# Ordering depthwise taps behind key chains, and moving seven taps per tile to ScalarE and adding transfers, in a two-layer hybrid trunk

## The chip, the core and the metric

The kernel runs on one core of one Trainium2 chip. The metric is device time in microseconds (us), lower is better. PE stands for TensorE (matrix products; PEld its weight loads), DVE for VectorE, ACT for ScalarE, POOL for GpSimd, SP for SyncE, which here only issues transfers.

## What is computed

Two layers (l = 0 and 1, "first" and "second" here) over 256 latent and 256 context tokens of 1024 channels, all in float32. The part of the reference that matters:

```python
h = modulate(rmsnorm(x, norm1_g[l]), sh1, sc1)
p = h @ w_in[l]                       # columns: GLU, q, k, v, gates
u = a * sigmoid(g)                    # conv_branch: a, g are the GLU halves, 512 channels
u = dwconv1d(u, dw, dw_b)             # centred depthwise convolution, width 31
u = silu(layernorm(u, ln_g, ln_b))
y_conv = u @ w_o
q, k = rope_2d(q), rope_2d(k)         # latent tokens only
y_attn = neighbourhood_attention(q, k, v, k_ctx, v_ctx, rpb) @ w_na_out
x = x + g1 * ((sigmoid(g_conv) * y_conv + sigmoid(g_attn) * y_attn) @ w_out)
h2 = modulate(rmsnorm(x, norm2_g[l]), sh2, sc2)
x = x + g2 * conv_ffn(h2)
```

Attention: four rows of 64 columns; a query sees the keys of a window of 16 columns in each row, and all 256 context keys. In the second layer the context tokens only give keys and values.

## The kernel before

**Weights and products.** Every float32 product is made of three products of two parts (`mm3`, L196 to L199): the weight's high part times the activation's high and low part, and the weight's low part times the activation's high part. A weight unit is a tile of 128 x 1024, 512 KB. `raw_unit` (L152) loads it by SP into one of four buffers `raw`; ACT rounds it into `whi` (L167, L216). The low part `wlo` is made in one of two ways: `wunit` has DVE subtract (L168); `wadded` (L211) has ACT write the negated high part (L217) and POOL issue a transfer that adds the raw tile into it (L218). The set `ADDED` (L47) names the units, by layer and unit number, that take the second way. In the second layer these are three: q tiles 1 and 2 and gate 2.

**Groups and slots.** Activations lie transposed: channels on the 128 partitions, tokens along the free dimension, 512 of them in the first layer (latent and context), 256 in the second. `group` (L201) makes one output tile of 128 channels in a PSUM bank of the pool "main" (four banks): 8 x 3 products. At its end, and for 512 tokens once in its middle, it calls `slot()` (L92), which advances every registered side job by one step. The side jobs are the convolution's taps, the attention's steps, the layer norm and the modulation's dot products.

**The convolution.** `glu` (L687) writes a padded tile `u` per 128 channels (four tiles, j = 0 to 3) and appends its 31 taps to the list `taps`. A tap (L667) is one DVE instruction over the tile: the first writes `cb[j]` with scale and bias (L671), the others multiply a shifted view of `u` by one weight per partition and add it into `cb[j]` (L673). `conv_run` takes `rate` (2 or 3) taps per slot. When attention is done, `layer_norm` (L938) takes the rest, 5 or 6 per slot, then adds the four tiles (L949 and L950, in the second layer on POOL; L951 on DVE), sums over partitions on PE (L955), centres (L958), squares (L352, L356), and makes the reciprocal root with PE (L370), DVE (L378), POOL (L380) and PE (L386). Its output feeds the branch products of `w_conv_out` (L996).

**Queries and keys.** `qk(j)` (L843) is called for four pairs of heads. For q, then for k, it makes a group, rotates the latent part (DVE: L859, L860, L861, then L864 for q or L869 for k) and splits the results into high and low part (ACT L881, DVE L882). Keys are stored in three ranges: context (256 elements, straight from PSUM), and two ranges of 4 rows x 40 columns = 160 elements each, for the left and right half of the queries, with the columns outside. So a key chain ends with three casts and three subtractions. The queue of DVE steps from L859 to the last L882 is called a chain here. After both, `att.pair` registers the pair; the score products (L495) follow in a later slot, then bias and row maximum (DVE L516), exponentials (ACT L519) and scaling (L522), transposition (PE L561, copied by ACT L564 or L567) and the values (PE L578, L587; ACT L595, DVE L596).

**Order.** Each engine runs its own instructions in order. That order is a plan made when the program is built: instructions are taken in the order in which the code creates them, but one that is expected to be ready may be put ahead of one that is expected to wait. `tc.issue_after(i)` ties what is created inside it behind instruction i on the same engine, without a wait. The variable `after` (L658) holds the instruction behind which later taps are tied: the scores' L516 (or L530) sets it, so that taps don't stand ahead of scores. Nothing ties taps to the query and key chains.

Of the kernel before, what the change touches and what calls it, by code (L numbers as in the profile page):

```python
# [8 lines left out]
F32 = mybir.dt.float32  # L9
# [3 lines left out]
ALU = mybir.AluOpType  # L13
AX = mybir.AxisListType

P = 128
# [27 lines left out]

U_GLU0, U_V, U_IN, U_NA, U_CO, U_WO, U_UP, U_DN = 0, 2, 6, 36, 40, 44, 52, 96
NU = 118
ADDED = {*((0, U_IN + i) for i in (*range(19), 20, 22, 24, 26, 28)), *((0, u) for u in (U_NA + 1, U_NA + 3, *range(U_CO, U_CO + 4))), *((1, U_IN + i) for i in (7, 8, 16))}  # L47
T_GLU, T_Q, T_K, T_GATE = 0, 6, 10, 14

SWAP16 = [(i + 16) % 32 for i in range(32)]  # L50

# [2 lines left out]
def trunk(ctx: ExitStack, tc: tile.TileContext, xt, cvec, crow, wall, wada, params, bias_t, rope_t, out):  # L54
# [368 lines left out]
    class Attention:  # L423
# [147 lines left out]
        def values(self, what, js, pT, bank):  # L571
# [19 lines left out]
            for n, j in enumerate(js):  # L591
# [3 lines left out]
                act.copy(to[0], src)  # L595
                dve.tensor_tensor(to[1], src, to[0].bitcast(F32), ALU.subtract)  # L596

    def blocks(ap):
        return ap.rearrange("p (r b c) -> p b r c", r=ROWS, b=NB_)

# [31 lines left out]
    for l in range(DEPTH):  # L632
# [5 lines left out]
        with ExitStack() if last else start as e1a:  # L638
# [19 lines left out]
            after = [None]  # L658

            def conv_tap(j, t):  # L660
                if after[0] is not None:
                    with tc.issue_after(after[0].ins):
                        tap(j, t)
                else:
                    tap(j, t)

            def tap(j, t):  # L667
# [4 lines left out]
                else:  # L672
                    dve.scalar_tensor_tensor(cb[j], src, w, cb[j], ALU.mult, ALU.add)  # L673

            rate = [0.0]

            def conv_run():
                due = 0.0
# [33 lines left out]

            with ExitStack() as e1b:
                eb = e1b.enter_context(tc.tile_pool(name=f"eb{l}", bufs=1))
                V = [eb.tile([P, CONV], F32, name=f"V{l}_{t}") for t in range(2)]
                VW = eb.tile([P, NB_, CONV], F32, name=f"VW{l}")
                att = Attention(l, eb, T, V, VW, oh, ol, after)
# [125 lines left out]
                def qk(j):  # L843

                    att.ahead(j - 2)
                    bt = eb.tile([P, 5, NS_ // 2], F32, tag="bias", bufs=2 if last else 1, name=nm("bias"))
                    both = []
                    for what in range(2):
                        w = T if what == 0 else 2 * S
                        sc = HD ** -0.5 if what == 0 else 1.0  # L850
                        ps = in_group((T_Q, T_K)[what] + j, slice(0, w))
                        if what == 0:
                            with tc.issue_after(lastdma[0].ins):
                                sp.dma_start(bt, bias_t[l, j])
                        r1, r2 = tmp(), tmp()
                        got = back(ps[:, :w])
                        lat, ctx_ = (got[:, 0], got[:, 1]) if w > S else (got, None)
                        part = halves if w == S else lambda a: a
                        dve.tensor_tensor(part(r1[:, LAT]), lat, part(rope[:, 0, :]), ALU.mult)  # L859
                        dve.stream_shuffle(part(r2[:, LAT]), lat, SWAP16)  # L860
                        dve.tensor_tensor(r2[:, LAT], r2[:, LAT], rope[:, 1, :], ALU.mult)  # L861
                        if what == 0:
                            rq = tmp()
                            dve.tensor_tensor(  # L864
                                rq[:, LAT].rearrange("p (b r c) -> p b r c", b=NB_, r=ROWS),
                                blocks(r1[:, LAT]), blocks(r2[:, LAT]), ALU.add,
                            )
                        else:
                            dve.tensor_tensor(r1[:, LAT], r1[:, LAT], r2[:, LAT], ALU.add)  # L869
                        f = eb.tile([P, 2, KN if what else w], F32R, tag="qk"[what], bufs=2, name=nm("qk"))  # L870
                        if what == 0:
                            to = [([f[:, a, LAT] for a in range(2)], rq[:, LAT])]
                            if T > S:
                                to.append(([f[:, a, CTX] for a in range(2)], ctx_))
                        else:
                            rv_ = r1[:, LAT].rearrange("p (r c) -> p r c", r=ROWS)
                            to = [([f[:, a, KCTX] for a in range(2)], ctx_)]
                            for d, c in ((slice(0, KL), slice(GW - TC, GW)), (slice(KX, KN), slice(0, TC))):
                                to.append(([f[:, a, d].rearrange("p (c r) -> p r c", r=ROWS) for a in range(2)], rv_[:, :, c]))
                        for (hi, lo), src in to:  # L880
                            act.activation(hi, src, AF.Identity, scale=sc)  # L881
                            end = dve.scalar_tensor_tensor(lo, src, sc, hi.bitcast(F32), ALU.mult, ALU.subtract)  # L882
                        both.append(f)
                    att.pair(j, *both, bt, end)

# [39 lines left out]
            with ExitStack() as e1c:  # L925
# [12 lines left out]
                def layer_norm():  # L938
# [5 lines left out]
                        yield  # L944
                    pace[0] = 1.0 if last else 1.2
                    flat = [c.rearrange("p s t -> p (s t)") for c in cb]
                    sm = tp.tile([P, 512], F32, tag="ss", name=nm("ss"))
                    eng = pool if last else dve
                    eng.tensor_tensor(sm[:, :T], flat[0], flat[1], ALU.add)  # L949
# [407 lines left out]
```

## Time and profile before

| what | value |
|---|---|
| median of 3 runs (lowest, highest) | 1058.18 us (1057.49, 1059.27) |
| profiled execution: time, span | 1054.58 us, 1052.8 us |
| granted PE clock, mean over the span | 0.997 |
| second layer's taps on DVE, first and last tile's first tap | 688.2 us, 791.2 us |

A line of the grouped view reads: source line, engine, operation, output <- inputs, shapes, count | busy us, mean ns of one | idle time of the engine just before, and what ended it. A line of the waits view reads: engine and line that waited <- engine and line that ended the wait: total us, times, longest. A line of the timeline reads: start us, duration us, engine, line, operation, names, shapes, count. A busy row by stretch reads: the stretch, its length, busy us (and count of instructions) of PE, PEld, DVE, ACT, POOL, then the granted PE clock, the mean busy share of the 16 DMA engines and GB/s. A line of transfers reads: names, issuing queue, operation, count, KB each, median us from issue to landing. In the view of one source line the three durations are shortest, median and longest in ns, then come the starts of the first and the last.

### The profile page before, as it was taken

The page shows a single profiled execution, that of the slowest core. Times are in us where ns is not written, and L with a number is a line of the kernel's source. Part 1 is how long each engine was busy: PE and PEld are TensorE (multiplying, and loading weights), DVE is VectorE, ACT ScalarE, POOL GpSimd, SP SyncE. Part 2 cuts the span into 40 slices and gives each one's busy share as a digit, 9 for nine tenths or more (in the row PEclk, how much of TensorE's full clock was granted, in tenths as well). Part 3 has the DMA queues.
Part 4 walks back from the last instruction along what each step waited for, and adds up shares of the span by engine and source line. Part 5 has one row for each costly group of instructions (what it writes and reads, how often), then busy time and mean ns, then how long its engine had stood idle before and what let it go on. Part 6 is the DMA issues. An engine that isn't in the chain of part 4 may idle for free.

```text
span 1052.8 us, 17991 instructions
## 1 busy us (share of the span) xinstructions
PE 1032.4 (98%) x6886; PEld 932.9 (89%) x6886; DVE 893.2 (85%) x1608; ACT 565.6 (54%) x921; POOL 43.7 (4%) x59
## 2 busy tenths in 40 slices
PE   9999999999999999999999999999999999999997
PEld 7787788888889988888888889999889999999996
DVE  6568899999998787878788888799899988988883
ACT  4458768545434644444444223545777666766652
POOL 1111110011000000000000000000000000000000
PEclk9999999999999999999999999999999999999998
DMA  9989674888945345454545887556734485666781
GB/s 374 305 221 229 156 181 121 258 255 236 305 146 177 104 140 160 140 164 143 166 145 160 301 289 249 180 189 209 208 123 135 161 292 176 193 201 199 221 283 57
DMA packets 59511, 209.26 MB, mean 199 GB/s; under 512 B 7201, under 2 KB 7457, under 8 KB 59425
## 3 DMA queue, kind: packets, MB, share of 16 engines
q1 hardware_dynamic: 54384, 190.77, 55.3%
q0 software_dynamic: 4752, 17.30, 8.7%
q8 instruction: 54, 0.88, 0.3%
q14 instruction: 33, 0.26, 0.1%
q10 hardware_dynamic: 288, 0.04, 0.0%
HBM read 187.63 MB, written 1.05 MB: 179 GB/s over the span
## 4 chain that ended last, share of the span: by engine, by line
PE 68%; DVE 17%; ACT 5%; DMA 4%; issue 3%; SPq 1%; DVEq 0%; ACTq 0%
PE main L197 20%; PE main L198 20%; PE main L199 20%; DVE cb L673 6%; PE main L736 4%; DVE wlo L168 3%; DMA raw<-in_wall 2%; DVE t L304 2%; DMA own<-in_wada 1%; SPq L728 1%; PE sc L197 1%; PE sc L199 1%; PE sc L198 1%; DVE qk L882 1%; ACT pp L519 1%
## 5 line engine op out<-in xcount | busy, mean ns | idle before, releaser
L197 PE MATMUL main<-h,whi 128*128 128x256 f32 (+1 forms) x1328 | 433.1, 326 | 1.2 <-DVE qk L882 1.2
L198 PE MATMUL main<-h,whi 128*128 128x256 f32 (+1 forms) x1328 | 430.2, 324 | 0.9 <-DVE h L1001 0.7
L199 PE MATMUL main<-h,wlo 128*128 128x256 f32 (+1 forms) x1328 | 429.9, 324 | 1.2 <-DVE wlo L168 1.1
L167 ACT CAST whi<-raw 128x1024 fp32r<-128x1024 f32 (+1 forms) x211 | 218.3, 1039 | 234.8 <-PE main L198 173.6
L168 DVE TENSOR_TENSOR wlo<-raw,whi 128x1024 fp32r<-128x1024 f32 (+1 forms) x211 | 253.6, 1208 | 67.2 <-ACT whi L167 66.4
L197 PEld LDWEIGHTS main<-h,whi 128*128 128x128 f32 x1328 | 252.8, 190 | 22.0 <-issue 1.3
L199 PEld LDWEIGHTS main<-h,wlo 128*128 128x128 f32 x1328 | 252.5, 190 | 18.5 <-DVE wlo L168 1.8
L198 PEld LDWEIGHTS main<-h,whi 128*128 128x128 f32 x1328 | 252.7, 190 | 18.3 <-DVE h L1001 1.0
L304 DVE CUSTOM_DVE_ANT_0 t<-own,sb,par 128x1024 bf16<-128x1024 f32 x120 | 151.8, 1282 | 6.8 <-DMA own<-in_wada 6.8
L673 DVE SCALAR_TENSOR_TENSOR cb<-u,par,cb 128x512 f32<-128x512 f32 (+1 forms) x240 | 144.7, 620 | 2.8
L198 PE MATMUL main<-fl,whi 128*128 128x256 f32 (+1 forms) x396 | 122.8, 310 | 0.0
L197 PE MATMUL main<-fh,whi 128*128 128x256 f32 (+1 forms) x396 | 122.8, 310 | 0.0
L199 PE MATMUL main<-fh,wlo 128*128 128x256 f32 (+1 forms) x396 | 122.5, 310 | 0.0
L197 PEld LDWEIGHTS main<-fh,whi 128*128 128x128 f32 x396 | 75.6, 191 | 3.8 <-ACT fh L1095 0.2
L198 PEld LDWEIGHTS main<-fl,whi 128*128 128x128 f32 x396 | 75.6, 191 | 3.7 <-DVE fl L1096 0.2
L199 PEld LDWEIGHTS main<-fh,wlo 128*128 128x128 f32 x396 | 75.5, 191 | 3.6
L216 ACT CAST whi<-raw 128x1024 fp32r<-128x1024 f32 x33 | 34.6, 1049 | 36.0 <-PE main L198 30.5
L404 ACT ACTIVATE h<-t,mod 128x256 fp32r<-128x256 f32 x56 | 25.2, 503 | 34.8 <-DVE t L403 34.3
L218 POOL DMA_DIRECT2D wlo<-raw x33 | 28.9, 877 | 258.9 <-ACT wlo L217 107.6
L736 PE MATMUL main<-whi,h 128*128 128x512 f32 x128 | 38.5, 386 | 0.2
L1105 ACT ACTIVATE t<-t 128x512 f32<-128x512 f32 x22 | 13.9, 632 | 41.3 <-DVE t L1074 41.3
L217 ACT ACTIVATE wlo<-whi 128x1024 fp32r<-128x1024 f32 x33 | 35.0, 1061 | 0.5
(214 smaller groups left out, 1268.8 us busy)
## 6 DMA issues: line engine op xcount, KB each, us to landing
raw<-in_wall SPq DMA_DIRECT2D x240, 512.0 KB, 4.3
own<-in_wada SPq DMA_DIRECT2D x72, 512.0 KB, 4.7
wlo<-raw POOLq DMA_DIRECT2D x33, 512.0 KB, 5.4
raw<-in_wada SPq DMA_DIRECT2D x16, 512.0 KB, 5.8
bias<-in_bias_t SPq DMA_DIRECT2D x8, 520.0 KB, 5.3
row<-in_wada SPq DMA_DIRECT2D x8, 512.0 KB, 5.1
sb<-in_crow SPq DMA_DIRECT2D x5, 512.0 KB, 4.8
x<-in_xt SPq DMA_DIRECT2D x4, 512.0 KB, 5.1
```

The costliest lines, as they stand in the source:

```text
L167: act.copy(hi[:, c], r[:, c])
L168: dve.tensor_tensor(lo[:, c], r[:, c], hi[:, c].bitcast(F32), ALU.subtract)
L197: pe.matmul(ps, w[0], order(xh), start=start, stop=False)
L198: pe.matmul(ps, w[0], order(xl), start=False, stop=False)
L199: pe.matmul(ps, w[1], order(xh), start=False, stop=stop)
L216: act.copy(hi, r)
L217: act.mul(lo, hi.bitcast(F32), -1.0)
L218: pool.dma_start(lo, r, accum_op=ALU.add)
L304: dve.tensor_tensor_reduce(tmp().bitcast(BF16), r, v, 1.0, pr(l, BADA + n, 1), ALU.mult, ALU.add, mods[l][:, n, s : s + 1])
L404: high = act.activation(hi[:, c], y[:, c], AF.Identity, bias=b)
L673: dve.scalar_tensor_tensor(cb[j], src, w, cb[j], ALU.mult, ALU.add)
L736: mm = pe.matmul(pv[t], h1[n == 1][k][:, c], runs(w[n == 2][:, b]), start=k + n == 0, stop=k == KD - 1 and n == 2)
```

## The change

Four edits:

1. In both layers `qk` sets `after` to the last DVE step of the q chain, and then of the key chain, so taps created later are tied behind it.
2. The two key ranges of 160 elements are cast and subtracted in one instruction each over 320, by a view with a step between the ranges (`steps`).
3. In the second layer, taps 1, 3, 5, 7, 9, 11 and 13 of each tile (`FAR`) leave DVE. ACT multiplies the shifted view by the weight; the first product of a tile is written to `far[j]`, each of the other six to one of 16 buffers `farq`, from where POOL issues a transfer of 128 KB that adds it into `far[j]`. Before the layer norm's sums DVE adds `far[j]` to each tile. The far taps are not tied behind `after`. They still count as taps at the slots.
4. The second layer's three units leave `ADDED`; DVE subtracts their low parts.

```diff
-ADDED = {*((0, U_IN + i) for i in (*range(19), 20, 22, 24, 26, 28)), *((0, u) for u in (U_NA + 1, U_NA + 3, *range(U_CO, U_CO + 4))), *((1, U_IN + i) for i in (7, 8, 16))}
+ADDED = {*((0, U_IN + i) for i in (*range(19), 20, 22, 24, 26, 28)), *((0, u) for u in (U_NA + 1, U_NA + 3, *range(U_CO, U_CO + 4)))}
+FAR = range(1, 14, 2)
...
+    def steps(a, first, *dims):
+        return bass.AP(tensor=a.tensor, offset=a.offset + first, ap=[a.ap[0], *dims])
...
             def conv_tap(j, t):
-                if after[0] is not None:
+                if last and t in FAR:
+                    far_tap(j, t)
+                elif after[0] is not None:
                     with tc.issue_after(after[0].ins):
                         tap(j, t)
...
+            far = {}
+            def far_tap(j, t):
+                w = par[:, l * NPAR + DW + j * TAPS + t : l * NPAR + DW + j * TAPS + t + 1]
+                src = us[j % NU_][:, 0, t : t + S]
+                if j not in far:
+                    far[j] = ea.tile([P, S], F32, name=f"far{l}_{j}")
+                    act.activation(far[j], src, AF.Identity, scale=w)
+                else:
+                    q = eb_[0].tile([P, S], F32, tag="farq", bufs=16, name=nm("farq"))
+                    act.activation(q, src, AF.Identity, scale=w)
+                    pool.dma_start(far[j], q, accum_op=ALU.add)
...
                         else:
-                            rv_ = r1[:, LAT].rearrange("p (r c) -> p r c", r=ROWS)
                             to = [([f[:, a, KCTX] for a in range(2)], ctx_)]
-                            for d, c in ((slice(0, KL), slice(GW - TC, GW)), (slice(KX, KN), slice(0, TC))):
-                                to.append(([f[:, a, d].rearrange("p (c r) -> p r c", r=ROWS) for a in range(2)], rv_[:, :, c]))
                         for (hi, lo), src in to:
                             act.activation(hi, src, AF.Identity, scale=sc)
                             end = dve.scalar_tensor_tensor(lo, src, sc, hi.bitcast(F32), ALU.mult, ALU.subtract)
+                        if what:
+                            hi, lo = (steps(f[:, a], 0, (KX, 2), (1, ROWS), (ROWS, TC)) for a in range(2))
+                            src = steps(r1, GW - TC, (TC - GW, 2), (GW, ROWS), (1, TC))
+                            act.copy(hi, src)
+                            end = dve.tensor_tensor(lo, src, hi.bitcast(F32), ALU.subtract)
+                        after[0] = end
...
                     flat = [c.rearrange("p s t -> p (s t)") for c in cb]
+                    for j in far:
+                        dve.tensor_tensor(flat[j], flat[j], far[j], ALU.add)
```

More of the change, by code (lines that the diff above doesn't have):

```diff
@@ L673, in tap @@
                     dve.scalar_tensor_tensor(cb[j], src, w, cb[j], ALU.mult, ALU.add)
+            far = {}
[9 more added lines that the diff above has]
+                    pool.dma_start(far[j], q, accum_op=ALU.add)
             rate = [0.0]
+            eb_ = [None]
             def conv_run():
@@ L714, in trunk @@
                 eb = e1b.enter_context(tc.tile_pool(name=f"eb{l}", bufs=1))
+                eb_[0] = eb
                 V = [eb.tile([P, CONV], F32, name=f"V{l}_{t}") for t in range(2)]
```

## The prediction

> **What bounds the kernel now.** I read the page's head first, then the waits of the matrix engine (PE) in the two stages that the change touches, then the busy time of the engines there, then the order of instructions around the waits.
>
> ```profile
> span 1052.8 us, 17991 instructions
> PE 1032.4 (98%) x6886; PEld 932.9 (89%) x6886; DVE 893.2 (85%) x1608; ACT 565.6 (54%) x921; POOL 43.7 (4%) x59
> ```
>
> PE is idle for 1052.8 - 1032.4 = 20.4 us of the whole span. No change that leaves the products alone can win more than the part of this that lies in its stages. The profiled execution took 1054.58 us, 3.60 below the median of 1058.18; I make the sum on the profiled one and carry the difference over.
>
> PE's waits from 75 to 300 us (first layer's attention and what follows) and from 690 to 890 us (second layer's):
>
> ```profile
> PE sc L495 <- ACT pT L567: 1.7, 1, 1.7
> PE po L955 <- DVE ss L951: 1.0, 1, 1.0
> PE sc L495 <- ACT qk L881: 0.9, 1, 0.9
> PE sc L495 <- DVE qk L882: 0.6, 1, 0.6
> ```
> ```profile
> PE pt L370 <- DVE ss L356: 1.8, 2, 1.0
> PE main L197 <- DVE qk L882: 1.2, 2, 0.6
> PE main L199 <- DVE wlo L168: 1.1, 2, 0.9
> PE sc L495 <- ACT pT L564: 0.2, 1, 0.2
> ```
>
> Columns: total us, times, longest. The change aims at the lines with qk: 0.9 + 0.6 = 1.5 us in the first layer, where score products wait for key halves, and 1.2 us in the second, where a PSUM bank is freed late because DVE reads the key group late. By way of DVE's load it may also reach the layer norm's waits (L951, L356). The whole prize is some 4 us, 0.4% of the time.
>
> Busy time by stretch (PE, PEld, DVE, ACT, POOL, clock, DMA share, GB/s):
>
> ```profile
> 110.00:215.00 105.00, 102.09 (x650) 85.13 (x649) 98.95 (x188) 71.73 (x147) 9.56 (x11) 1.00 0.69 179
> 690.00:745.00 55.00, 55.00 (x359) 50.56 (x358) 51.67 (x117) 28.51 (x43) 2.65 (x3) 1.00 0.63 194
> 745.00:813.00 68.00, 66.61 (x639) 60.78 (x638) 66.37 (x161) 49.23 (x107) 2.31 (x2) 1.00 0.50 150
> ```
>
> DVE is full: 98.95 of 105 us, then 66.37 of 68. ACT and POOL are not. The clock is at 1.00 in all three, so no time is won there.
>
> **The change, part by part.**
>
> *Taps behind the chains, first layer.* The DVE order around the 1.5 us wait:
>
> ```profile
> 92.40 0.42 DVE L859 TENSOR_TENSOR t<-main,rope 128x256 f32<-128x256 f32 x1
> ...
> 93.09 0.74 DVE L673 SCALAR_TENSOR_TENSOR cb<-u,par,cb 128x512 f32<-128x512 f32 x1
> 93.74 0.42 DVE L861 TENSOR_TENSOR t<-t,rope 128x256 f32<-128x256 f32 x1
> ...
> 94.41 0.42 DVE L869 TENSOR_TENSOR t<-t,t 128x256 f32<-128x256 f32 x1
> 94.74 1.54 DVE L673 SCALAR_TENSOR_TENSOR cb<-u,par,cb 128x512 f32<-128x512 f32 x2
> 96.20 0.81 DVE L882 SCALAR_TENSOR_TENSOR qk<-t,qk 128x160 fp32r<-128x160 f32 x2
> ```
> ```profile
> 94.79 0.38 PE L199 MATMUL main<-h,wlo 128*128 128x512 f32 x1
> 96.04 0.44 PE L495 MATMUL sc<-qk,qk 64*128 64x416 f32 x2 [0.87 <-ACT qk L881]
> ```
>
> The key chain runs from 92.40 to 96.20 + 0.81 = 97.01. Three taps stand in it; by start times they take 93.74 - 93.09 = 0.65 and 96.20 - 94.74 = 1.46, together 2.11 us. Queued behind the chain they let it end at 97.01 - 2.11 = 94.90. PE's last product before the scores ends at 94.79 + 0.38 = 95.17, so the 1.5 us wait disappears. The same holds for the q chains, but nobody waits for those at present.
>
> What is late next: the taps themselves. They are queued in the place they lose, and the layer norm stands behind the last tap: PE already waits 1.0 us there (L955 <- L951). From 110 us on DVE has 105.00 - 98.95 = 6.05 us to spare until then, so PE's 1.5 us is kept only as far as DVE uses such gaps. Against it, a chain pauses twice while ACT casts a high half (latent and context), which taps used to fill; I bound a pause by 0 and 0.5 us (a cast takes 0.62, below, and part of it lies beside the next DVE step), so the four chains of head pairs 2 and 3, all after 110 us, cost DVE 0 to 4 x 2 x 0.5 = 4.0 us. First layer: 1.5 won at best, 4.0 lost at worst; I take -0.7, nearer the gain, since DVE's 6.05 us cover the pauses.
>
> *Both key ranges at once.* Durations (us busy, mean ns), the next fence over 690 to 813 us, the one after it over the whole run:
>
> ```profile
> L673 DVE SCALAR_TENSOR_TENSOR cb<-u,par,cb 128x256 f32<-128x256 f32 x118 | 54.7, 489 | 1.2
> L168 DVE TENSOR_TENSOR wlo<-raw,whi 128x1024 fp32r<-128x1024 f32 x27 | 32.9, 1224 | 0.5 <-ACT whi L167 0.5
> L881 ACT ACTIVATE qk<-t 128x160 fp32r<-128x160 f32 x8 | 4.4, 620 | 1.1 <-DVE t L869 1.1
> ```
> ```profile
> L217 ACT ACTIVATE wlo<-whi 128x1024 fp32r<-128x1024 f32 x33 | 35.0, 1061 | 0.5
> L218 POOL DMA_DIRECT2D wlo<-raw x33 | 28.9, 877 | 258.9 <-ACT wlo L217 107.6 <-DVE cb L673 41.6 <-ACT qk L881 36.1
> L356 DVE TENSOR_TENSOR ss<-ss,t 128x256 f32<-128x256 f32 x44 | 18.1, 422 | 4.6 <-ACT t L352 4.4
> L882 DVE SCALAR_TENSOR_TENSOR qk<-t,qk 128x160 fp32r<-128x160 f32 x16 | 7.8, 531 | 0.3
> L1199 ACT ACTIVATE x<-x,par 128x256 f32<-128x256 f32 x8 | 4.0, 497 | 5.0 <-DVE x L1007 5.0
> ```
>
> Two pieces of 160 elements become one of 320. On DVE the pair takes 0.81 us in the order above; one of 320 lies between the 0.42 of a plain 256 there and that 0.81. I take 0.6, so 0.2 us is saved per key chain on DVE, eight times, and by analogy as much on ACT. That is 1.6 us of DVE time over both layers; its place is inside the chains and I count it there.
>
> *Three weight units back to DVE.* For q tiles 1 and 2 and gate 2 of the second layer a negated copy on ACT (1.061) and an accumulating transfer from POOL (0.877 to issue) go, and a DVE subtraction (1.224) comes: DVE +3.7, ACT -3.2 us. They keep POOL's queue free for what follows.
>
> *Seven taps per tile.* From DVE go 28 x 0.489 = 13.7 us; four additions come, 4 x 0.422 = 1.7. With the units: -13.7 + 3.7 + 1.7 = -8.3 us of 51.67 + 66.37 = 118.0 in 123 us, so DVE falls from 96% to 89%. ACT gets 28 products; the row of a scaled 128x256 is L1199's 0.497: +13.9 - 3.2 = +10.7 us on 28.51 + 49.23 = 77.7, from 63% to 72%. ACT's work fills idle time; it is at nothing as long as exponentials and score copies come first, and costs up to one product (0.5 us) each time one stands ahead of them: PE's 0.2 us wait for pT would grow.
>
> *24 accumulating transfers.* Of one tile's seven products one is written and six are added into the same buffer, so each addition waits for the landing of the one before, and POOL's queue, in order, holds everything else behind it: the next tile's additions, L949, L950 and the layer norm's power L380. No row shows 128 KB (128 x 256 x 4 bytes) accumulated; the nearest:
>
> ```profile
> wlo<-raw POOLq DMA_DIRECT2D x33, 512.0 KB, 5.4
> out<-t SPq DMA_DIRECT2D x2, 128.0 KB, 1.8
> ```
> ```profile
> L693 DVE SCALAR_TENSOR_TENSOR u<-t,sc x2: 414/552/690, 57.8 to 687.7; 128x512 f32<-128x512 f32 x1, 128x256 f32<-128x256 f32 x1
> L693 DVE SCALAR_TENSOR_TENSOR u<-t,main x6: 415/555/694, 80.6 to 735.2; 128x512 f32<-128x512 f32 x3, 128x256 f32<-128x256 f32 x3
> ```
> ```profile
> 812.96 0.42 DVE L951 TENSOR_TENSOR ss<-ss,cb 128x256 f32<-128x256 f32 x1
> ```
> ```profile
> 816.51 0.60 PE L955 MATMUL po<-ss,one 128*128 128x256 f32 x2
> ```
>
> A step lies between 1.8 us (the size, as a plain write) and 5.4 us (the operation, at four times the size). I take the middle, 3.6. The first tile's input is there at 687.7 + 0.4 = 688.1, the fourth's at 735.6; 24 x 3.6 = 86.4, so the last addition lands near 774.5, long before the layer norm's first full sum at 812.96. Price on the path: nothing, with 38 us of cover.
>
> [...]
>
> *Second layer, sum.* With 8 us less on DVE and no tap inside a chain, I let the bank waits shrink from 1.2 to 0.4 us and the layer norm's 1.0 (the longest of L370) to 0.2. The 1.1 us of L168 lies at 840 us, behind the stage, and stays. That is -1.6. With the first layer: -1.6 - 0.7 = **-2.3 us**: 1054.58 - 2.3 = 1052.3 profiled, **1055.9** as a median. A measurement of this kernel tells about 0.2%, 2.1 us, from no change.
>
> **Rivals.**
> - *Nothing to measure.* The bank waits follow the DVE's score rows and weight splits, which stay, as much as the taps; and the first layer's 1.5 us comes back at L955 because DVE is full. For it: 98.95 of 105. Against it: 6 us of gaps. Then -1 to +1: about 1058.
> - *Additions too late (slower).* If a step takes what a 512 KB one takes, 24 x 5.4 = 129.6, the last lands at 817.7; then come the fourth DVE addition and L951, 0.42 each: 818.5, and PE, which takes it at 816.51, waits 2.0 us. DVE, in order, is held from 812.96 to 817.7, 4.7 us, with weight splits behind it. Price 2.0 to 4.7, say 3.4, less the first layer's 0.7: 1060.9. It decides from a step of (816.5 - 0.8 - 688.1) / 24 = 5.3 us. Against it: 512 KB must be four times the data.
> - *First layer's taps late (slower).* The pauses cost nearly all, 3.5 of the 4.0 us, at L955, and the 1.5 us are spent there too; with the second layer's gain halved: +3.5 - 0.8 = +2.7, 1060.9. It decides where pauses pass 2.9 us (2.1 + 0.8). For it: DVE at 94% there. Against it: the gaps, and 0.2 us saved per chain.
>
> That the change does not do what it says: taps already traced before a chain may still stand in it, since only later ones are tied to its end. That leads to the first rival.
>
> **How the numbers follow.** Forecast with both gains 0.46, own range 1053.5 to 1056.0; nothing 0.31; additions late 0.10; taps late 0.13. The likeliest gives 1055.9. Faster 0.46, same 0.31, slower 0.23. The best end takes all reachable waits (1.5 + 1.2 + 1.0 + 1.0 = 4.7) and a little more for re-ordering: 1052.5. The upper end holds both slower rivals: 1061.0.
>
> **What would show it.** Right: no L673 between L859 and L882; the waits L495 <- qk gone and L197 <- qk under 0.5; L951 done before 812.96; 24 POOL additions that end before 790. Wrong: POOL additions up to 810, a DVE wait on a DMA in front of an addition, PE's wait at L955 grown to 2 us and more in the first layer, or PE waiting for pT in the second.

## The result and the profile after

The changed kernel takes 1063.37 us (median of 6 runs, 1062.49 to 1064.54), the kernel before beside it 1057.84 (6 runs, 1055.06 to 1059.76). The ratio is 1.0054, 95% interval 1.0037 to 1.0070: 0.54% slower, 5.5 us, where 0.2% faster was forecast and 1061.0 was the upper end. The profiled execution took 1062.64 us, 8.1 more than that of before, which was a fast one, 3.3 us under the median beside it; so lags between the two traces overstate the loss by 2.5 us.

The head of the page, after:

```profile
span 1060.8 us, 18028 instructions
PE 1035.4 (98%) x6886; PEld 934.2 (88%) x6886; DVE 891.6 (84%) x1579; ACT 573.9 (54%) x938; POOL 64.4 (6%) x80
```

PE does the same 6886 products and is busy for 3.0 us more. DVE lost 1.6 us, not 8. So time went in two ways: PE waits longer, and its products themselves are slower somewhere.

PE's waits after, from 75 to 300 us and from 690 to 890 us (L497 to L983 are the former L495 to L955, moved by the new lines; L563 is the transposition, L524 the scaling of the exponentials, L566 and L569 the copies of pT, L906 and L907 the joint cast and subtraction):

```profile
PE sc L497 <- ACT pT L569: 1.4, 1, 1.4
PE pt L563 <- ACT pp L524: 1.3, 1, 1.3
PE sc L497 <- ACT qk L906: 1.3, 1, 1.3
PE po L983 <- DVE ss L979: 1.0, 1, 1.0
...
PE sc L497 <- DVE qk L907: 0.4, 1, 0.4
```
```profile
PE main L201 <- DVE wlo L170: 2.4, 3, 0.9
PE pt L563 <- ACT pp L524: 1.4, 1, 1.4
PE pt L497 <- ACT pT L566: 1.3, 1, 1.3
```

The wait for key halves, the first layer's prize, is 1.3 + 0.4 = 1.7 us where it was 1.5. The waits for a bank that DVE's qk holds are gone in the second layer, as forecast. New in both layers is a wait of the transpositions for the exponentials, 1.3 and 1.4 us, and in the second one for pT, 1.3. The wait for weight splits (L170, the former L168) is 2.4 us where it was 1.1.

Busy time by stretch, of the changed kernel behind the two new waits, then of before at the first place:

```profile
106.00:110.00 4.00, 3.83 (x38) 2.70 (x40) 2.24 (x4) 3.99 (x9) 0.25 (x1) 0.57 0.63 229
...
758.00:762.00 4.00, 4.00 (x13) 2.88 (x12) 4.00 (x8) 2.11 (x7) 0.86 (x1) 0.57 0.47 145
```
```profile
106.00:110.00 4.00, 3.73 (x49) 3.18 (x44) 1.83 (x5) 2.73 (x6) 0.88 (x1) 1.00 0.71 230
```

The column behind POOL is the granted PE clock: 0.57 in both. Behind each new wait it is 0.50 in the rows of 1 us from 107 to 109 us and from 759 to 761, and by the rows around them for 3.4 us in all; this is called half clock below. At 758 us PE did 13 products in 4 us.

Where the 8.1 us lie is read by setting the same product of PE's order side by side in the two traces (its start before, its start after, the difference): 96.04, 96.27, 0.2; 103.96, 106.11, 2.2; 105.85, 109.03, 3.2; 128.60, 131.19, 2.6; 179.01, 183.46, 4.5; 291.72, 296.60, 4.9. Nothing is added up to 735 us. Then 750.52, 757.16, 6.6; 753.07, 761.43, 8.4; 761.65, 768.68, 7.0; 770.09, 779.09, 9.0; 821.98, 828.78, 6.8; 863.67, 871.96, 8.3, and nothing from there on. So the first layer lost 4.9 us, 4.5 of them in its attention, and the second's attention about 2 net, with 1.5 more at 863 us, where two weight splits came late.

The first new wait begins on DVE:

```profile
92.72 0.42 DVE L882 TENSOR_TENSOR t<-main,rope 128x256 f32<-128x256 f32 x1
93.06 0.74 DVE L681 SCALAR_TENSOR_TENSOR cb<-u,par,cb 128x512 f32<-128x512 f32 x1
...
95.00 0.42 DVE L902 SCALAR_TENSOR_TENSOR qk<-main,qk 128x256 fp32r<-128x256 f32 x1
96.25 0.76 DVE L907 TENSOR_TENSOR qk<-t,qk 128x320 fp32r<-128x320 f32 x1 [0.83 <-ACT qk L906]
96.91 3.90 DVE L681 SCALAR_TENSOR_TENSOR cb<-u,par,cb 128x512 f32<-128x512 f32 x5
100.73 0.59 DVE L518 CUSTOM_DVE_ANT_0 sc<-sc,bias 128x416 f32<-128x416 f32 x1
```

The chain ends at 97.01, as before, and not at 94.90. It starts 0.32 us later, since two taps that were tied to the query chain's end stand ahead of it (one did before); one tap still stands in it; and at its end DVE is idle for 0.83 us, where a tap used to run. Five taps now stand behind the chain and ahead of the first score row (three before), so that row starts at 100.73 instead of 99.16. Exponentials follow the rows, transpositions the exponentials.

### The profile page after: what moved, and what is told of

The parts are those of the page before. It is cut to its first block, busy times and chain, and to the rows that moved or that the text cites. A ratio compares the mean times of both kernels' runs of the same rounds, so it can differ in the third digit from the quotient of the medians.

```text
span 1060.8 us, 18028 instructions
## 1 busy us (share of the span) xinstructions
PE 1035.4 (98%) x6886; PEld 934.2 (88%) x6886; DVE 891.6 (84%) x1579; ACT 573.9 (54%) x938; POOL 64.4 (6%) x80
## 4 chain that ended last, share of the span: by engine, by line
PE 69%; DVE 17%; ACT 5%; DMA 5%; issue 2%; SPq 1%; DVEq 0%; ACTq 0%
PE main L199 20%; PE main L200 20%; PE main L201 20%; DVE cb L681 5%; PE main L759 4%; DMA raw<-in_wall 3%; DVE wlo L170 3%; DVE t L306 2%; DMA own<-in_wada 1%; SPq L751 1%; PE sc L199 1%; PE sc L201 1%; PE sc L200 1%; PE po L232 1%; ACT whi L169 1%
## 5 line engine op out<-in xcount | busy, mean ns | idle before, releaser
L169 ACT CAST whi<-raw 128x1024 fp32r<-128x1024 f32 (+1 forms) x214 | 221.0, 1037 | 234.9 <-PE main L200 176.2
L170 DVE TENSOR_TENSOR wlo<-raw,whi 128x1024 fp32r<-128x1024 f32 (+1 forms) x214 | 256.7, 1206 | 71.2 <-ACT whi L169 70.8
L681 DVE SCALAR_TENSOR_TENSOR cb<-u,par,cb 128x512 f32<-128x512 f32 (+1 forms) x212 | 134.0, 635 | 4.0
L218 ACT CAST whi<-raw 128x1024 fp32r<-128x1024 f32 x30 | 31.4, 1048 | 35.6 <-PE main L200 28.9
L220 POOL DMA_DIRECT2D wlo<-raw x30 | 26.3, 876 | 208.4 <-ACT wlo L219 107.8
L382 POOL TENSOR_TENSOR rs<-red,mhalf 128x2 f32<-128x2 f32 (+1 forms) x8 | 7.3, 908 | 496.8 <-DVE red L380 496.8
```

Source lines behind the costliest of these rows:

```text
L169: act.copy(hi[:, c], r[:, c])
L170: dve.tensor_tensor(lo[:, c], r[:, c], hi[:, c].bitcast(F32), ALU.subtract)
L218: act.copy(hi, r)
L220: pool.dma_start(lo, r, accum_op=ALU.add)
```

## The experiments

All times are medians, and a ratio is that to the kernel before on the same chip, with its 95% interval. The kernel before took 1056.17 to 1057.39 us there, so 0.001 is 1.06 us.

**The parts one by one.** Theory T, the tie (first edit); J, the joint key ranges (second); F, far taps and units (third and fourth).

e1_tie, the tie alone:

```diff
+                        after[0] = end
                         both.append(f)
```

> The kernel before with the taps tied behind query and key chains, nothing else. Theory T (the tie bunches taps behind a chain, they stand ahead of the score rows, the exponentials and with them PE's transposes come late): 3 to 5 us slower than before, with a wait of 1 us or more of PE for the scaled exponentials near 102 us and products at double spacing behind it. Theory J (the joint key ranges, a cast that waits for the subtraction before it and takes as long as two) and theory F (far taps and three units on DVE): within 1 us of before.

Measured: 1063.04 us, 1.0062 (1.0050 to 1.0075), 6.6 us slower. Its trace has a wait of 1.30 us for L522 at 106.17 us and products at half speed behind it: the eight of L578 at 107.33 us take 1.97 us, as in the changed kernel, where those of the kernel before took 1.08. Theory T holds.

e2_joint, the joint key ranges alone:

```diff
...
+                        if what:
+                            hi, lo = (steps(f[:, a], 0, (KX, 2), (1, ROWS), (ROWS, TC)) for a in range(2))
+                            src = steps(r1, GW - TC, (TC - GW, 2), (GW, ROWS), (1, TC))
+                            act.copy(hi, src)
+                            end = dve.tensor_tensor(lo, src, hi.bitcast(F32), ALU.subtract)
```

> The kernel before with both key ranges in one cast and one subtraction, nothing else. Theory J: 2 to 5 us slower, since the key chain waits for the context's subtraction. Theories T and F: within 1 us of before.

Measured: 1058.76 us, 1.0029 (1.0014 to 1.0043). So J costs too, 3.1 us by the ratio. The view of the cast's line shows the mechanism that J names (what the engine waited for in front of it: us, times):

```profile
L906 ACT CAST qk<-t x8: 769/960/1102, 71.1 to 783.2; 128x320 fp32r<-128x320 f32 x8
...
its engine sat idle before it (us, times) until:
  DVE qk L902: 5.3, 4
```

The joint view steps over the context range that lies between the two ranges, and the cast is held until DVE has read the context's high half, though they share no element. (Before, the casts of 160 waited for L869 alone.) But the way from there to 3 us isn't closed: in this trace most of the loss is a stretch of half clock from 129.7 to 136.4 us (granted clock 0.56 from 129.5 to 133.0, 0.50 from there on) behind a wait of 2.0 us that was 1.7 before, and the last section shows that such a stretch stands behind that wait in some traces and not in others.

e3_far, the second layer's part alone (third and fourth edit):

```diff
-                if after[0] is not None:
+                if last and t in FAR:
+                    far_tap(j, t)
+                elif after[0] is not None:
...
+                    for j in far:
+                        dve.tensor_tensor(flat[j], flat[j], far[j], ALU.add)
```

> The kernel before with the second layer's part alone: seven taps per tile by ScalarE and adding transfers, and the three units back on DVE; no tie, no joint key ranges. Theory F: 3 to 5 us slower, with the stall of PE near 756 us and the late weight splits near 871 us. Theories T and J: 0 to 2 us faster, as the bank waits and the layer norm's wait of 1 us go.

Measured: 1054.06 us, 0.9988 (0.9966 to 1.0011). Theory F falls: its stall at 756 us isn't there, only the late weight splits at 862 to 864 us (1.2 us). Whether the kernel is faster than before, this run leaves open; v1 below repeats it.

e4_no_tie, the changed kernel without the tie:

```diff
-                        after[0] = end
```

> The changed kernel without the tie. Theory T: at the time of before or up to 2 us faster, so 5 us below the changed kernel, with no stall near 102 us. Theories J and F: as slow as the changed kernel, 1063 us, give or take 1 us.

Measured: 1056.71 us, 1.0000 (0.9989 to 1.0011). The tie is the whole loss; the other edits together come out even.

**Where the tie costs.** f1_tie_first and f2_tie_second, the tie in one layer (f2 has `if last:`):

```diff
+                        if l == 0:
+                            after[0] = end
```

> The kernel before with the tie in the first layer alone. If the two layers' losses are separate, as e1's lag of 4.6 us up to 320 us and 4.5 us from 750 to 890 us suggests: 3 to 5 us slower than before, and nothing from 320 us on.

> The kernel before with the tie in the second layer alone: 2 to 5 us slower than before, all of it between 750 and 890 us. With the tie in the first layer alone it adds up to e1's 6.6 us. If the loss came from a run's chance alone, neither would be slower.

Measured: f1 1058.50 us, 1.0013 (1.0001 to 1.0024); f2 1061.67 us, 1.0043 (1.0030 to 1.0057). They add up to e1 within their intervals, but not by halves: 1.4 us by the ratio for the first layer, less than expected, and 4.5 for the second. f1's trace has the same wait of 1.30 us near 106 us as e1's and a granted clock of 1.00 behind it, and the same product that e1 starts 4.6 us late near 297 us starts 4.9 us late in f1 (297.78 against 292.85). These lags are set against the traced execution of before, 1054.58 us, which is 2.8 us under the median beside f1; so they overstate the first layer's loss.

f3_tie_key, the tie behind key chains alone, in both layers:

```diff
+                        if what:
+                            after[0] = end
```

> The kernel before with the taps tied behind the key chains only, in both layers. The order of DVE then has no tap in the first key chain and eight of them, 5.9 us, between it and the first score row (before: three in the chain, three behind it). Theory T (taps bunched ahead of score rows): PE's 1.5 us wait for the key halves goes, but the score rows come later than in e1, so 3 to 8 us slower than before. Theory P (the loss is the pauses of the chains, which taps no longer fill): query chains keep their taps, so half of e1's loss or less, 1 to 3 us.

Measured: 1061.16 us, 1.0046 (1.0028 to 1.0064), and the prize was won all the same. DVE and PE's longest wait there:

```profile
95.39 0.82 DVE L882 SCALAR_TENSOR_TENSOR qk<-t,qk 128x160 fp32r<-128x160 f32 x2 [0.43 <-ACT qk L881]
96.12 4.68 DVE L673 SCALAR_TENSOR_TENSOR cb<-u,par,cb 128x512 f32<-128x512 f32 x6
100.72 0.59 DVE L516 CUSTOM_DVE_ANT_0 sc<-sc,bias 128x416 f32<-128x416 f32 x1
```
```profile
PE pt L561 <- ACT pp L522: 1.3, 1, 1.3
...
PE sc L495 <- ACT qk L881: 0.2, 1, 0.2
```

No tap stands in this chain, it ends at 96.2, and PE waits 0.2 us for key halves instead of 1.5. Six taps follow, and the score row comes at 100.72. PE gives the gain back at the transpositions. That all of it is lost there isn't shown: the second layer's key tie, which f3 has too, costs 3.7 us alone (n3 below), so the first layer's share of f3's 4.9 is about 1 us, within the intervals.

g1_hold, e1 and, in the first layer, taps held in a list from a key chain until its score rows are queued:

```diff
             def conv_tap(j, t):
+                if hold[0]:
+                    held.append((j, t))
+                    return
...
```

> The tie of e1 in both layers, and in the first layer the taps that fall between a key chain and its score rows are held until those score rows are queued. The order of DVE has no tap in the first key chain and none between it and the four score rows. Theory T: the first layer at the time of before or 1 to 2 us under it, so only the second layer's 2 to 4.5 us remain over before. Theory P: chains pause as in e1, so 6 to 7 us slower, as e1.

Measured: 1071.88 us, 1.0143 (1.0127 to 1.0160), a miss for both theories. The held taps, freed behind one pair's rows, stand one by one between the steps of the next pair's chains, from 88 to 101 us:

```profile
PE sc L497 <- ACT qk L895: 3.0, 1, 3.0
...
PE sc L497 <- DVE qk L896: 1.8, 1, 1.8
```

It doesn't clear T of the first layer, as meant. It shows that on a full DVE a tap kept out of one place stands in another, and that PE waits 4.8 us for a chain full of taps. Where the rest of g1's 15 us went was not followed.

**How the second layer loses.** In f2 DVE is idle three times in a row, twice until an exponential is there and once until the tied chain's cast is, with taps waiting that nothing but the tie holds back:

```profile
751.98 0.16 DVE L521 RECIPROCAL ri<-sm 128x1 f32<-128x1 f32 x1 [0.93 <-ACT pp L519]
752.57 0.16 DVE L521 RECIPROCAL ri<-sm 128x1 f32<-128x1 f32 x1 [0.43 <-ACT pp L519]
...
754.02 1.11 DVE L882 SCALAR_TENSOR_TENSOR qk<-t,qk 128x160 fp32r<-128x160 f32 x2 [0.59 <-ACT qk L881]
```
```profile
PE main L197 <- ACT pp L519: 2.7, 1, 2.7
```

Theory H: these 1.95 us and the taps that are made up for later delay the next rows. Theory B: PE's 2.7 us are for a PSUM bank that the key group of the last pair of heads is given. The order of PE's instructions, with the engines that each waits for, has for that group's first product (before, then f2):

```
4104 L197 MATMUL main_1307_7652<-h_926_5468,whi_1309_7654 128x512 [waits DVE_49,PE_49]
4104 L197 MATMUL main_1307_7652<-h_926_5468,whi_1309_7654 128x512 [waits Activation_49]
```

m1_mid, the second layer's tie, to the rotation's last addition instead of the chain's end (the query chain's likewise):

```diff
-                            dve.tensor_tensor(r1[:, LAT], r1[:, LAT], r2[:, LAT], ALU.add)
+                            mid = dve.tensor_tensor(r1[:, LAT], r1[:, LAT], r2[:, LAT], ALU.add)
+                        if last:
+                            after[0] = mid
```

> The tie in the second layer alone, as in f2, but to the last addition of the rotation instead of the last subtraction of the chain, so that taps may run while ScalarE casts the high halves. Theory H (the tie holds taps back while DVE waits for ScalarE, 1.95 us near 752 us in f2, and they then stand ahead of the next score rows): most of f2's 4.3 us goes, 0 to 1.5 us over before. Rival (any tie bunches the taps as badly): 3 to 5 us slower, as f2.

Measured: 1058.84 us, 1.0021 (1.0009 to 1.0034): half of f2's loss, between the two expectations. It doesn't speak for H alone, since its trace has f2's wait too, one pair of heads earlier (it ends at 750.97 us, and the granted clock is 0.50 in the rows from 751 to 754 us behind it):

```profile
PE main L197 <- ACT pp L519: 2.6, 1, 2.6
```

d1_delay, no tie, but late score rows:

```diff
+                if self.l and it[0] == 1 and not qt and i == 0:
+                    for _ in range(4):
+                        late = dve.tensor_copy(self.eb.tile([P, 512], F32, tag="late", bufs=1, name=nm("late"))[:, :NS_], ps)
+                    with tc.issue_after(late.ins):
+                        self.after[0] = dve.tensor_tensor_reduce(p2, p2, b2, -1.0, 3.0e38, ALU.add, ALU.min, mx)
```

> The kernel before, no tie, with four idle copies of DVE of some 0.45 us ahead of the first score row of the second layer's second pair of heads; the order lets three chain steps of 0.42 us pass with them, so the row comes about 3 us later. The output is that of the reference; only idle work is added. If PE has no slack against late score rows (f2: rows 1.5 us later against PE, and a wait 2.1 us longer): 2 to 3.5 us slower, with PE's wait for the exponentials (L519's line) near 762 us. If rows have slack: under 0.5 us.

Measured: 1058.06 us, 1.0015 (1.0000 to 1.0029), between the two expectations. The row (L520 here) starts at

```profile
768.05 0.59 DVE L520 CUSTOM_DVE_ANT_0 sc<-sc,bias 128x416 f32<-128x416 f32 x1
```

PE starts these score products 6.5 us behind the trace of before (760.32 against 753.85), and the row was at 758.11 there, so it comes 3.5 us later against PE. Yet PE has no wait for L519's line here, only 0.9 us at the transpositions. In f2 the row comes at 762.59 with PE 3.0 us behind (756.85), 1.5 us later against PE, and PE waits 2.7. Late rows alone are not it: PE's group had kept the bank that DVE frees.

n2_query_second and n3_key_second, the second layer's tie behind query chains or key chains alone (n3 has `if last and what:`):

```diff
+                        if last and not what:
+                            after[0] = end
```

> The kernel before with the tie behind the second layer's query chains alone. Theory B (the tie makes the key group's bank come free later in the planned order, so that the next key group is given a bank that waits for an exponential): 1.5 to 3 us slower, with PE's wait for L519 of 2 us or more near 764 us, since the order on PE names ScalarE as what that group waits for, as in f2. Theory H (taps held back behind the key chain's end): 0 to 1 us slower, since the key chains are not tied.

> The kernel before with the tie behind the second layer's key chains alone. Theories B and H: 3 to 5 us slower, as f2. If only both ties together cost: 1 us or less.

Measured: n2 1058.73 us, 1.0014 (1.0002 to 1.0026), n3 1060.51 us, 1.0035 (1.0022 to 1.0048). Both have the wait for L519, 1.1 and 2.0 us, and in both orders that group waits for Activation (ScalarE). So both theories have a part: the tie moves the bank (B), also where only query chains are tied, and how long PE then waits follows the rows (H): the pair's last score row starts at 762.59, 764.74 and 765.44 us in n2, n3 and f2, and PE's wait ends 2.1, 2.3 and 2.2 us later. The shares of the two in the time were not separated.

All this is the tie in the kernel before. The changed kernel's trace has no wait for L521, the former L519. What its second layer shows is the wait for L524 near 756 us, which e3, e4 and n1 below, without that tie, don't have. In it six taps stand on DVE between the end of a query chain and the last score row of the pair ahead, in n1 none does (first the changed kernel, then n1):

```profile
745.86 1.52 DVE L681 SCALAR_TENSOR_TENSOR cb<-u,par,cb 128x256 f32<-128x256 f32 x3
...
749.27 0.48 DVE L681 SCALAR_TENSOR_TENSOR cb<-u,par,cb 128x256 f32<-128x256 f32 x1
...
752.95 0.63 DVE L518 CUSTOM_DVE_ANT_0 main<-main,bias 128x416 f32<-128x416 f32 x1
```
```profile
750.23 0.57 DVE L518 CUSTOM_DVE_ANT_0 main<-main,bias 128x416 f32<-128x416 f32 x1
```

The last row starts at 752.95 instead of 750.23, while PE begins the transpositions at 754.63 and 754.76.

n1_after_first, the changed kernel with the tie in the first layer alone:

```diff
-                        after[0] = end
+                        if l == 0:
+                            after[0] = end
```

> The changed kernel with the tie in the first layer alone. If the second layer's tie is the loss in the changed kernel too: e4's 0 and f1's 1.1 add up to about 1 us over before, 5 us under the changed kernel. If the loss needs the first layer's tie or the joint ranges beside it: 3 us or more over before.

Measured: 1060.26 us, 1.0040 (1.0020 to 1.0061), with runs from 1057.3 to 1068.5. By the ratio that is 4.2 us over before, the second case: the first layer's tie costs more beside the other edits than alone, and the second layer's tie adds only 1.5 us to it here (1.0054 - 1.0040), which the intervals don't tell from nothing. Its trace has the wait of 1.3 us near 106 us, as the changed kernel's, and a mean clock of 0.993 over the span (0.994 there). Why the shares of the layers change over, stays open.

**What the other edits are worth.** v1_far has e3's edit once more:

> The second layer's part alone once more (far taps and three units on DVE, as e3), for a closer interval: 1 to 2.4 us under before if the bank waits and the layer norm's wait that go are a gain in every execution; within 1 us of before if e3's median was chance.

Measured: 1054.51 us, 0.9979 (0.9963 to 0.9995). It beats both kernels, by 2.2 us and, by the ratios, 8 us. The late weight splits of e3's trace are not in this one of the same kernel, so they are no price of the edit. What the far taps cost is there, a wait for pT:

```profile
PE pt L497 <- ACT pT L566: 1.4, 1, 1.4
PE main L201 <- DVE wlo L170: 0.9, 1, 0.9
```

e7_far, the far taps without the fourth edit, so with the three units left in `ADDED`:

```diff
-ADDED = {..., *((0, u) for u in (U_NA + 1, U_NA + 3, *range(U_CO, U_CO + 4)))}
+ADDED = {..., *((0, u) for u in (U_NA + 1, U_NA + 3, *range(U_CO, U_CO + 4))), *((1, U_IN + i) for i in (7, 8, 16))}
```

> The kernel before with the far taps of the second layer alone; the three weight units stay on ScalarE and POOL. If the units on DVE were what made weight splits late near 863 us in e3: 1 to 2 us under before and no such wait. If not: as e3, 0 to 2.4 us under before, or slower where 27 accumulations of two kinds share POOL's queue.

Measured: 1067.74 us, 1.0108 (1.0090 to 1.0126), the last of the three cases. PE's longest wait, and POOL's queue ahead of it:

```profile
PE main L201 <- DMA wlo<-raw: 10.0, 1, 10.0
```
```profile
734.23 0.87 POOL L694 DMA_DIRECT2D far<-farq  x1 [2.60 <-issue]
738.83 0.86 POOL L694 DMA_DIRECT2D far<-farq  x1 [3.73 <-DMA far<-farq]
739.46 1.12 POOL L220 DMA_DIRECT2D wlo<-raw  x1
```

A weight unit's accumulation stands behind far additions, and the last of them had waited 3.73 us for the landing of another. The three units on DVE are no side edit. They are what makes the far taps pay, by 1.0108 - 0.9979 = 0.0129, 13.6 us.

**The half clock.** h2_fill, the changed kernel with nine idle products in its two new waits:

```diff
...
+                if what == LAT and n == 1 and its[0][0] == 1 - self.l:
+                    for _ in range(9):
+                        pe.matmul(sl(raw[1], 0), ident, ident, start=True, stop=True)
```

> The changed kernel with nine idle products of 128x128, about 1.2 us, put into PE's waits of 1.3 us at 106 us and 1.4 us at 756 us; nothing else. Theory C (an idle PE lets the granted clock fall to a half for one stretch of 3.4 us behind each, 1.7 us each): no half clock behind these two places and up to 3.4 us less than the changed kernel, so 1060 to 1062 us. If the half clock has nothing to do with the wait: at the changed kernel's 1063 us.

Measured: 1066.69 us, 1.0096 (1.0080 to 1.0112). There is no half clock behind the two places (the mean clock is 0.996 over the span), but the products also moved the planned order of the other engines, PE waits 2.4 and 0.8 us at 780 to 782 us instead, and there the clock is halved (0.50 in the rows from 783 to 785 us). It meets neither expectation and gives no price for the half clock.

c1_gaps and c2_filled put waits where PE has none:

```diff
+            def gap(n, fill):
+                ...
+                    mm = pe.matmul(sl(p, t), ident, ident, start=True, stop=True)
+                act.copy(g, p[:, :256])
+                for _ in range(n):
+                    act.copy(g, g)
+                ...
+                return pe.matmul(sl(p, 0), sl(g, 0), ident, start=True, stop=True)
```

> The kernel before with twenty waits of PE put into the first layer's feed-forward stage (360 to 570 us, where PE never waits): PE hands a tile to ScalarE, which copies it 1, 2, 4, 6 or 8 times, and takes it back before the next products; only idle work is added. The waits should be of about 0.7 to 4 us. Theory C (a wait lets the granted clock fall): no half clock behind waits under 1.2 us, and behind longer ones, more often the longer they are, stretches of half clock of some 3.4 us, 1.7 us lost in each; the time is the waits' sum and 1.7 us for each stretch. Rival (the half clock comes by itself): stretches have no relation to the waits, or none fall there.

> As c1, with twenty waits of one length (six copies, about 3 us), and in every second one sixteen idle products of 128x128, about 2 us of PE's work, at its start. Theory C: half clock behind the empty waits, none or few behind the filled ones. Rival: no difference between the two kinds.

Measured: c1 1174.16 us, c2 1190.82 (two runs each). Three of c1's waits, and the 4 us behind each (timeline, then stretches):

```profile
415.01 0.49 PE L1128 MATMUL po<-ident,gap 128*128 128x128 f32 x2 [2.08 <-ACT gap L1120]
...
460.75 0.49 PE L1128 MATMUL po<-ident,gap 128*128 128x128 f32 x2 [4.26 <-ACT gap L1122]
...
509.29 0.80 PE L1128 MATMUL po<-ident,gap 128*128 128x128 f32 x2 [2.52 <-ACT gap L1122]
```
```profile
415.20:419.20 4.00, 4.00 (x20) 3.54 (x20) 4.00 (x8) 0.75 (x2) 0.00 (x0) 1.00 0.35 131
...
509.70:513.70 4.00, 4.00 (x15) 3.33 (x15) 4.00 (x7) 1.25 (x2) 0.00 (x0) 0.67 0.40 126
...
461.00:465.00 4.00, 4.00 (x13) 3.19 (x13) 3.42 (x6) 0.85 (x2) 0.00 (x0) 0.57 0.12 37
```

The waits came out longer than meant; the shortest is 2.08 us, so c1 does not test the 1.2 us of Theory C. In the changed kernel's trace half clock follows waits of 1.3 and 1.4 us and, the span's last 6 us aside, none of up to 1.0. Of c1's four waits of 2.08 us none was followed by half clock, of the four of 2.52 us three, of the 12 of 3.39 us and more all. In c2, behind an empty wait of 4.26 us and behind one filled with products, of which 0.69 us was left:

```profile
398.20:402.20 4.00, 4.00 (x11) 3.21 (x11) 3.26 (x6) 0.70 (x2) 0.00 (x0) 0.50 0.10 25
...
415.90:419.90 4.00, 4.00 (x20) 3.53 (x20) 3.44 (x6) 0.90 (x2) 0.00 (x0) 1.00 0.12 19
```

So it was at all ten empty and all ten filled ones. In c2's stage of dense products the idle PE brings the half clock about, and products without use keep it away.

## Why the prediction was wrong

The step that failed is the pricing of the tie. The sum has it as a gain in both layers (-0.7 us in the first, a share of -1.6 us in the second); it costs 6.6 us alone (e1), and without it the changed kernel is at the time of before (e4).

*Taps behind the chains, first layer.* It was put as "Queued behind the chain they let it end at 97.01 - 2.11 = 94.90". That subtracts the taps' durations from the chain and leaves all else in its place. In the changed kernel the chain ends at 97.01: of its three taps one stayed in it, one more than before stands in front of it and two more behind, and 0.83 us is DVE idle while ACT casts. The prediction had bounded these pauses by 0 to 0.5 us each and charged them to the layer norm at the end of the stage, with 6.05 us of gaps as cover. The layer norm's wait is 1.0 us as before; the price came at once, at the next score row. The prediction asked who waits for the moved taps (the layer norm, in the end), but not who stands behind them in DVE's queue: the next chain, and the score rows. In f3, where the chain does end early, PE's wait for key halves falls by 1.3 us, a new wait of 1.3 us stands at the transpositions, and nothing is won. The first layer's tie costs 1.4 us alone (f1, 0.1 to 2.5) and 4.2 us in the changed kernel (n1, 2.1 to 6.4).

*The second layer's tie.* Of this the sum has only "no tap inside a chain", as a gain. Alone it is the larger loss, 4.5 us (f2); in the changed kernel it adds about 1.5 us to n1, not clear of the intervals. In f2 it comes by held-back taps and by a bank that now waits for an exponential; in the changed kernel's trace there is no such wait, and the taps ahead of the score rows go with the transpositions' wait of 1.4 us. Nothing in the working asked what the tie does to DVE's idle time there, or to the order in which banks come free.

*Joint key ranges.* 0.6 us was taken for 320 elements; the first layer's took 0.76 and the median of all eight is 0.96, about as long as two of 160 (0.81 in the first layer). The saving of 0.2 us per chain isn't there, and the cast's wait for the context's subtraction had not been seen. Alone the edit costs 3.1 us (1.0029).

*Units, taps and additions.* These steps held in the main. DVE falls by 893.2 - 887.3 = 5.9 us in e3 (8.3 forecast), in the changed kernel only by 1.6. A far transfer took

```profile
far<-farq POOLq DMA_DIRECT2D x24, 128.0 KB, 4.1
```

4.1 us to land, where 3.6 had been taken. The last was issued at 772.7 us, so it landed near 777, and the layer norm had them all: the rival of late additions fell. Only the first tile's addition on DVE stood too early in its queue and held DVE for 2.2 us at 718 us, where PE had no wait. ACT's products were not for nothing: the wait for pT grew from 0.2 to 1.3 us, more than the half microsecond allowed. The gain of 1.6 us for the second layer agrees with v1's 2.2 (0.5 to 3.9), though the terms differ, so the agreement is partly luck: in v1's trace the bank waits are gone (1.2 us) and the layer norm's falls from 1.8 to 0.6, against 1.2 us more for pT, and v1 has no tie, which the forecast counted into this gain.

*The rivals.* The one that was slower by way of the first layer's taps named the right edit and the wrong place (L955, where the wait is 1.0 us as before). "The change does not do what it says" was right in that a tap stays in the chain, but was given to the case without effect.

*The size.* Even with the right waits the sum would have been short. Two waits of 1.3 and 1.4 us, with transpositions of 64 columns on both sides, were each followed by half clock: eight products in a row, up to the one that starts at 761.43 us (753.07 before), lost 0.21 us each, 1.7 us. A wait was priced at its own length.

## What to carry to other kernels

On an engine that is full, ordering work behind a chain doesn't take it out of the way: ask which queue entry comes next behind the point of release, who waits for that one, and whether the engine has anything else to do while the chain itself waits for another engine. Judge an ordering edit from the planned order, engine by engine, and look there also for buffers and banks that change hands. Price a wait of PE with the clock that it may cost behind it: here up to 1.7 us (3.4 us at half clock) behind the waits of 1.3 and 1.4 us in the changed kernel's attention and nothing behind one of 2.7 us in f2's; among the dense products of c1 nothing behind 2.08 us, and up to 1.7 us behind three of four waits of 2.52 us.

## What the hardware showed

A wait of PE can cost more than its length. In rows of 1 us each, the granted clock of c1 and c2 is 1.00 or 0.50, but for the rows in which it changes. In c1 it fell to 0.50 for 3.4 us, up to 1.7 us lost, at ten of the eleven waits of 2.5 to 4.3 us, and for 3.4 or 6.8 us at those of 4.9 and 5.5 us; behind 2.08 us it did not fall. In c2 it was 6.8 us at every empty wait, those of 4.26 us too, part of it within the wait. The same wait may or may not cost. One of 1.1 to 2.3 us for L567's copies near 130 us stands in 18 of the traces here; in 8 of them half clock follows (e2: a wait of 2.0 us, a clock of 0.56 and 0.50 behind it), in 10 not (the changed kernel: 1.4 us, a clock of 1.00 from 126 to 134 us). What decides it was not shown. Times of one kernel differ too: of the 26 runs of the kernel before beside e1 to e4, the three with a mean clock of 0.993 or 0.994 took 1059.0 to 1061.0 us, the other 23 took 1054.4 to 1058.2.

Not of the chip, but of the plan: two views that share no element put one engine behind the other, as it seems because one steps over the other's range (5.3 us of ACT's idle time in e2).
